# Expert stage of a two-block transformer kernel: TensorE in program order, its parts reordered, output product in quarters, token low parts on POOL

## The chip, the cores and the metric

The kernel runs on one core of one Trainium2 chip. The metric is the time of one execution on the device in microseconds (us), from the first to the last instruction and what lies around it. Its engines work side by side: TensorE (PE) does matrix products and transposes, VectorE (DVE) and ScalarE (ACT) work element by element, GpSimd (POOL) does a few elementwise operations and issues small loads, SyncE (SP) issues the loads of the weights.

## The reference

256 tokens of width 1024 go through two blocks of two layers each. A layer of the first block is: a scale and a shift made from a condition vector (adaLN), a mixer of attention, retention and mLSTM, an output product, a layer norm, and a mixture of 16 experts of which each token takes two; then a second layer norm. A layer of the second block is another mixer and a dense feed-forward part, and at its end a gated product of the layer's own input `p` (`ple`). The change lies in the first block:

```python
mod = (c_act @ w_ada[l] + b_ada[l])[:, None, :]
sh_m, sc_m, g_m, sh_f, sc_f, g_f = jnp.split(mod, 6, axis=-1)
...
x = layer_norm(DEEPNORM_ALPHA * x + (1.0 + g_m) * mix, ln_mix_g[l], ln_mix_b[l])
h = x * (1.0 + sc_f) + sh_f
...
hid = jax.nn.silu(jnp.einsum('td,edf->tef', h, w_gate)) * jnp.einsum('td,edf->tef', h, w_up)
hid = hid * gate[:, :, None].astype(hid.dtype)
return jnp.einsum('tef,efd->td', hid, w_down)
...
e = p[l] @ w_ple_up[l]
```

## The kernel before

Tokens lie in two halves `t` of 128, widths in two halves `c` of 512. Products that must be exact take a value as a high and a low part: `split` (L382) makes the high part on ACT and subtracts it from the value on DVE.

The class `Flow` (`te`) issues every matmul (L88) and transpose (L92). Pieces of work that may be mixed in are generators started with `te.start`; each `te.tick()` in a loop lets them run on as far as a planned time (the number that they yield) allows, and `te.settle` runs one to its end. A scheduler then orders each engine's instructions once more, by priorities, among those that are ready by its own estimate; on PE the order of the code is not binding. Buffers are handed out in the order of the code.

The weights come through `Stream`: SP loads them in a fixed order of use into a ring of ten buffers (`wf`) of 1 MB each; a buffer comes free when the code calls `free` or `free_raw` and PE has read it. A layer's experts take 48 such pieces.

A layer of the first block ends its mixer with `out_product` (L911), which sums four parts of the mixed values into two accumulators for each token half, and calls `done(t, c, ps)` for each finished quarter. `done` (L1131) makes the residual and the statistics, and behind the second quarter of a half the layer norm, and starts `moe_enter`: it transposes the normed tokens, multiplies them by the router, and keeps them as high and low parts (L1188 to L1192). Routing and ranking give each token its slot: an expert has 64 slots, two experts make a pair `q`, and a pair has 128 rows. A branch leaves for a slow way if a token has no slot.

Then the expert stage of `moe` follows. `gather(h)` brings the tokens into the slots (eight groups of four matmuls); `slots` transposes the slot matrix `P` to `PT`; `up(q)` multiplies the pair's rows by gate and up weights, 16 matmuls in which the pair's two experts alternate on two halves of 64 columns each; the result is gated to `hid` on ACT and DVE; `turn` transposes `hid` to `d`; `down(q)` is eight matmuls of the same alternating kind; `add(q)` brings the result, as high and low parts `yh` and `yl`, back to the tokens with eight matmuls. In before the loop runs up(q), down(q-1), turn, while add is a task that waits for 4.2 planned us and is then mixed in matmul by matmul. In layer 1 a further task, `ple_up(1)` (L1528), multiplies the loaded `p` by its weights; it belongs to the second block and stores its result by an SP DMA. `leave` ends the stage with the second layer norm.

Of the kernel before, what the change touches and what calls it, by code (L numbers as in the profile page):

```python
# [72 lines left out]
class Flow:  # L73
# [4 lines left out]
    def __init__(self, tc):  # L78
        self.tc, self.now, self.tasks, self.inside = tc, 0.0, [], False

# [3 lines left out]
    def matmul(self, out, lhsT, rhs, us=None, **k):  # L84
        if us is None:
            us = math.prod(rhs.shape[1:]) * (4 if rhs.dtype == F32 else 1) / 2400.0
        self.spend(max(us, 0.027))
        return self.tc.nc.tensor.matmul(out, lhsT, rhs, **k)  # L88

    def transpose(self, out, src, ident):  # L90
        self.spend(0.107)
        return self.tc.nc.tensor.transpose(out, src, ident)  # L92
# [113 lines left out]
class Build:  # L206
    def __init__(self, tc, A, out, es):
# [11 lines left out]
        self.NB4 = 13  # L219
        self.stream = Stream(self, 10, 4, 6)  # L220
# [301 lines left out]
    def ada(self, n):  # L522
# [3 lines left out]
        for _ in range(n):  # L526
# [18 lines left out]
            if k0 == 6:  # L545
                end = self.te.start(self.ada_end(l, r, row))
        return end
# [147 lines left out]
    def mix1(self, l, hs, done):  # L695
        nc = self.nc
        te, tick = self.te, self.tick
        with ExitStack() as es:
# [202 lines left out]
            return self.out_product(("out", l), mixh, mixl, (0, 1, 3, 2), lambda q: te.settle(need[q]), done)  # L901
# [9 lines left out]
    def out_product(self, key, mh, ml, order, need, done):  # L911
# [211 lines left out]
    def block1(self, l, hs):  # L1123
# [7 lines left out]
        def done(t, c, ps):  # L1131
# [3 lines left out]
            if t == 0 and c == 0:  # L1135
                e.gB = [self.bcast(self.gate[l][i]) for i in range(2)]
                self.router(l, e)
                e.lg = self.sc([128, 2, 16])
                e.xT = [None, None]
                e.xs, e.back = [], []  # L1140
# [10 lines left out]
        self.mix1(l, hs, done)  # L1151
# [13 lines left out]
    def moe_enter(self, l, e, t, xn):  # L1165

        nc, te = self.nc, self.te
        yield 4.6 if t == 0 else 0.5
# [20 lines left out]
        for c in range(2):  # L1189
            cs = slice(512 * c, 512 * c + 512)  # L1190
            self.split(h[:, cs], lw[:, cs], xn[:, cs])
        e.xs.append((h, lw))  # L1192

    def back(self, l, e, t):
# [8 lines left out]
        for k in range(8):  # L1203
            te.matmul(e.out[t][k // 4][:, spread(k % 4)], e.xT[t][:, k], self.identa,
                      start=k % 4 == 0, stop=False)
            if k == 3:
                yield 1.6

# [81 lines left out]
    def moe(self, l, e, xn):  # L1290
# [4 lines left out]
        with ExitStack() as es:  # L1295
# [37 lines left out]
            gather(0)  # L1333
            gt = self.gates(e)
            gsp = self.sc([128, 8, 2])
            for q in range(8):
                for t in range(2):
                    te.matmul(gsp[:, q], P[t].bitcast(F32)[:, q * 128:(q + 1) * 128], gt[:, t, 2 * q:2 * q + 2],
                              start=t == 0, stop=t == 1)
            gsl = S([128, 8], "m_gsl")  # L1340
            for a in range(2):
# [676 lines left out]
```

## Time and profile before

| | |
|---|---|
| time, median of 3 runs | 1476.96 us (1475.59 to 1484.74) |
| profiled execution, its own time | 1477.39 us |
| its span, first to last instruction | 1475.6 us |
| mean granted TensorE clock | 0.963 of full speed |
| PE busy | 1381.2 us, 94% |
| DVE busy | 879.1 us, 60% |
| ACT busy | 657.7 us, 45% |
| POOL busy | 83.2 us, 6% |
| DMA, mean over the span | 216 GB/s |

The first block fills the span to about 790 us, its two expert stages lie at 254 to 406 and at 618 to 778. The second block takes the rest. How it is read: the page gives the busy share of each engine; the timeline lists instructions in order with the idle time ahead of each and the engine that ended it; a table of stretches gives busy time, granted clock and DMA rate between two times. On PE consecutive rows overlap a little, since the matmuls are pipelined, and each matmul of full-precision inputs of `up` and `down` stands twice, once for each of its passes.

### The profile page before, as it was taken

Reading aid. Unit: us, or ns where it says so; the run is one execution under the profiler, and the core shown is the slowest. Engines: PE = TensorE matmul, PEld = TensorE weight load, DVE = VectorE, ACT = ScalarE, POOL = GpSimd, SP = SyncE. Lnnn points to the kernel's source line nnn. Section 1 sums busy time; section 2 is a strip of 40 time slices with the busy share of each in tenths; the row PEclk is TensorE's granted clock in tenths of the full one; section 3 lists DMA queues with packets and bytes.
Section 4 is the critical chain, followed back from the end, with each engine's and each line's share of the span. In section 5 each row is a group of like instructions: output and inputs, shape, how many; then the busy total and the mean of one; then the engine's idle time right before and its main releaser. Section 6 shows DMA issues by size and latency. Waiting matters only on the chain.

```text
span 1475.6 us, 18521 instructions
## 1 busy us (share of the span) xinstructions
PE 1381.2 (94%) x6642; PEld 972.5 (66%) x6642; DVE 879.1 (60%) x2094; ACT 657.7 (45%) x1317; POOL 83.2 (6%) x107
## 2 busy tenths in 40 slices
PE   4899997999979999799998998999999999999997
PEld 1667676633356767563336886888877887788885
DVE  1787567121288776412228787655569787665567
ACT  1536233111233542411116756555467866555554
POOL 3210001100001010000002000000001000000000
PEclk7899997999989999899999999999999999999999
DMA  9776597399746666539956533565655543556550
GB/s 334 250 270 217 211 327 286 127 411 412 253 171 235 228 220 243 200 118 410 411 222 225 177 95 128 167 191 184 193 176 166 176 119 114 171 172 193 188 204 28
DMA packets 129887, 318.12 MB, mean 216 GB/s; under 512 B 10199, under 2 KB 67711, under 8 KB 119546
## 3 DMA queue, kind: packets, MB, share of 16 engines
q1 hardware_dynamic: 125546, 304.96, 58.5%
q0 software_dynamic: 4240, 11.88, 2.7%
q8 instruction: 56, 0.92, 0.3%
q14 instruction: 45, 0.37, 0.1%
HBM read 313.64 MB, written 3.17 MB: 215 GB/s over the span
## 4 chain that ended last, share of the span: by engine, by line
PE 47%; DVE 6%; ACT 3%; issue 1%; DVEq 0%; ACTq 0%
PE sc L88 22%; PE mm L88 17%; PE tp L88 6%; PE tp L92 3%; DVE w L368 3%; ACT w L367 1%; DVE b L1603 0%; ACT junk L1599 0%; DVE b L1611 0%; ACT qz L693 0%; DVE b L384 0%; DVE rs_t L403 0%; DVE y L1401 0%; ACT b L383 0%; DVE b L1511 0%
## 5 line engine op out<-in xcount | busy, mean ns | idle before, releaser
L88 PE MATMUL mm<-w,b 128*128 128x512 f32 (+3 forms) x1920 | 454.6, 384 | 7.1 <-DVE b L601 4.1
L88 PEld LDWEIGHTS mm<-w,b 128*128 128x128 f32 x1920 | 342.7, 192 | 72.7 <-issue 8.1
L88 PE MATMUL sc<-w,b 128*128 128x512 f32 x1056 | 251.8, 394 | 3.7 <-DVE b L384 3.2
L368 DVE SCALAR_TENSOR_TENSOR w<-wf,vt,w 128x512 fp32r<-128x512 f32 (+2 forms) x304 | 199.3, 705 | 48.7 <-ACT w L367 48.5
L88 PEld LDWEIGHTS sc<-w,b 128*128 128x128 f32 x1056 | 197.1, 189 | 45.3 <-DVE b L384 4.1
L367 ACT ACTIVATE w<-wf,vt 128x512 fp32r<-128x512 f32 (+2 forms) x304 | 188.9, 681 | 46.8 <-PE sc L88 18.3
L362 DVE TENSOR_TENSOR w<-wf,w 128x1024 fp32r<-128x1024 f32 (+1 forms) x140 | 168.7, 1224 | 42.0 <-ACT w L361 41.5
L361 ACT CAST w<-wf 128x1024 fp32r<-128x1024 f32 (+1 forms) x140 | 140.7, 1033 | 71.4 <-PE mm L88 36.6
L88 PE MATMUL tp<-wf,X 128*64 128x512 f32 x512 | 132.9, 616 | 0.0
L88 PE MATMUL mm<-w,fh 128*128 128x512 f32 x352 | 110.5, 395 | 0.0
L88 PEld LDWEIGHTS tp<-wf,X 128*64 128x64 f32 x512 | 37.2, 140 | 70.3 <-issue 67.7
L88 PE MATMUL sc<-wf,d 128*64 128x512 f32 x256 | 79.2, 599 | 0.0
L1370 DVE SCALAR_TENSOR_TENSOR hid<-hid,m_gsl,tp 128x256 f32<-128x256 f32 x16 | 7.7, 481 | 119.7 <-ACT hid L1369 119.7
L88 PEld LDWEIGHTS mm<-w,fh 128*128 128x128 f32 x352 | 64.6, 188 | 12.5
L88 PE MATMUL mm<-w,fl 128*128 128x512 f32 x176 | 68.7, 390 | 0.0
L92 PE MATMUL tp<-identr,b 128*128 128x128 f32 (+3 forms) x236 | 40.3, 307 | 29.9 <-DVE b L1515 13.7
L1369 ACT ACTIVATE hid<-tp 128x256 f32<-128x256 f32 x16 | 6.1, 384 | 138.1 <-PE tp L88 138.1
L88 PE MATMUL sc<-wf,cact 128*32 128x512 f32 x384 | 53.0, 653 | 13.0 <-DMA wf<-in_w_ada_dram 9.1
L1895 DVE SCALAR_TENSOR_TENSOR f<-sc,en_r,sl 128x256 f32<-128x256 f32 x44 | 21.2, 481 | 68.4 <-ACT sl L1893 68.4
L92 PEld LDWEIGHTS tp<-identr,b 128*128 128x128 f32 (+3 forms) x236 | 31.1, 167 | 45.1 <-DVE b L1515 15.4
L1893 ACT ACTIVATE sl<-sc,en_r 128x256 f32<-128x256 f32 x44 | 20.5, 465 | 80.5 <-PE sc L88 80.5
L88 PE MATMUL sc<-b,b 128*128 128x512 f32 x128 | 41.4, 466 | 11.9 <-DVE m_gsum L1279 4.7
(402 smaller groups left out, 1649.9 us busy)
## 6 DMA issues: line engine op xcount, KB each, us to landing
wf<-in_w_ada_dram SPq DMA_DIRECT2D x48, 1024.0 KB, 6.9
wf<-in_w_ffn_in_dram SPq DMA_DIRECT2D x88, 512.0 KB, 4.8
wf<-in_w_in_dram SPq DMA_DIRECT2D x32, 1024.0 KB, 6.1
wf<-in_w_gate_dram SPq DMA_DIRECT2D x64, 512.0 KB, 7.6
wf<-in_w_up_dram SPq DMA_DIRECT2D x64, 512.0 KB, 8.8
wf<-in_w_down_dram SPq DMA_DIRECT2D x32, 1024.0 KB, 9.5
wf<-in_w_ffn_out_dram SPq DMA_DIRECT2D x22, 1024.0 KB, 4.9
wf<-in_w_out_dram SPq DMA_DIRECT2D x12, 1024.0 KB, 7.1
```

Of the source, the lines that this page charges most:

```text
L88: return self.tc.nc.tensor.matmul(out, lhsT, rhs, **k)
L92: return self.tc.nc.tensor.transpose(out, src, ident)
L361: nc.scalar.copy(wh, w)
L362: nc.vector.tensor_tensor(wl, w, wh, OP.subtract)
L367: nc.scalar.activation(wh[:, k], w[:, k], AF.Copy, scale=g)
L368: nc.vector.scalar_tensor_tensor(wl[:, k], w[:, k], g, wh[:, k], op0=OP.mult, op1=OP.subtract)
L1369: nc.scalar.activation(hid, gu[:, 0], AF.Silu)
L1370: nc.vector.scalar_tensor_tensor(hid, hid, gsl[:, q:q + 1], gu[:, 1], op0=OP.mult, op1=OP.mult)
L1893: nc.scalar.activation(sl, gu[:, :256], AF.Silu, scale=r)
L1895: nc.vector.scalar_tensor_tensor(f, gu[:, 256:], r, sl, op0=OP.mult, op1=OP.mult)
```

## The change

Five things are done, all in the first block.

- `Flow` has a switch `strict`. While it is on, `behind` makes each PE instruction depend on the one issued before it, so the scheduler keeps the order of the code on PE. It is on from the first gather to the last add of each expert stage.
- The code of the stage is reordered. The slot gates come behind up(0) instead of behind gather(0). For each q the order is up(q), down(q-1), add(q-2), turn; for q = 1 slots take the place of the add. add is no task any more: its eight matmuls stand together, by token halves, and the elementwise part that makes `yh` and `yl` stands in down. At the end come down(7), add(6), add(7), and in layer 1 ple_up(1) is started only then.
- `out_product` finishes its last two parts quarter by quarter for both token halves (before: one half at once, then two quarters), and frees the last weights later.
- A hook `before` runs ahead of these quarters: it settles the adaLN tasks that are still open, and makes the broadcasts and the router's operands, which `done` made in its first call.
- `moe_enter` makes the low parts of the tokens by a POOL subtract instead of DVE's, and yields 2.4 planned us instead of 4.6. `warm` is added and not called.

```diff
+    def behind(self, made):
+
+        if self.strict and self.last:
+            self.tc.add_manual_dep(made.ins, self.last, mybir.DependencyInfo(
+                mybir.DependencyClass.NoSync, mybir.DependencyReason.DATA))
+        self.last = made.ins.name
+        return made
...
-        part(2, 0)
-        part(3, 0)
-        done(0, 0, ps[0])
-        done(0, 1, ps[0])
-        for c in range(2):
-            part(2, 1, (c,), c == 1)
-            part(3, 1, (c,), c == 1)
-            done(1, c, ps[1])
+        if before:
+            before()
+        for t in range(2):
+            for c in range(2):
+                part(2, t, (c,), t == 1 and c == 1)
+                part(3, t, (c,), t == 1 and c == 1)
+                done(t, c, ps[t])
...
+        def before():
+            te.settle(*self.ada_ends)
+            e.gB = [self.bcast(self.gate[l][i]) for i in range(2)]
+            self.router(l, e)
...
-        yield 4.6 if t == 0 else 0.5
+        yield 2.4 if t == 0 else 0.5
...
-            self.split(h[:, cs], lw[:, cs], xn[:, cs])
+            nc.scalar.copy(h[:, cs], xn[:, cs])
+            nc.gpsimd.tensor_tensor(lw[:, cs], xn[:, cs], h[:, cs], OP.subtract)
...
-                return te.start(add(q))
-
-            def add(q):
-
                 yh, yl = self.b4([128, D], F32R), self.b4([128, D], F32R)
...
-                yield 4.2
+                ys[q] = yh, yl
+
+            def add(q):
+
                 for t in range(2):
                     for c in range(2):
                         cs = slice(512 * c, 512 * c + 512)
-                        for y in (yh, yl):
+                        for i, y in enumerate(ys[q]):
                             te.matmul(out[t][c], PT[:, q, t * 128:(t + 1) * 128], y[:, cs], start=False,
...
+            te.strict = True
+            gather(0)
             for q in range(8):
-                hid = up(q)
+                gu = up(q)
                 if q == 0:
+                    slot_gates()
+                    hid = gated(q, gu)
                     slots((0, 2))
                     gather(1)
-                elif q == 1:
-                    slots((4, 6))
-                    self.rows(l, x)
-                if q:
-                    end = down(q - 1, d)
+                else:
+                    hid = gated(q, gu)
+                    down(q - 1, d)
+                    if q == 1:
+                        slots((4, 6))
+                        self.rows(l, x)
+                    else:
+                        add(q - 2)
                 d = turn(hid)
...
-            end = down(7, d)
+            down(7, d)
+            add(6)
+            add(7)
+            te.strict = False
             fill = te.start(self.ple_up(1), 1) if l else None
-            te.settle(end)
```

Three places show how instructions stand in a row. The first is PE in layer 0's expert stage, one of the later pairs. `tp<-wf,X` are matmuls of an up, `sc<-wf,d` of a down, `tp<-identr,hid` the two transposes of a turn, `mm<-b,PT` the adds into four accumulators. Before:

```order
L88 MATMUL tp<-wf,X 64x512 x15
L88 MATMUL sc<-wf,d 64x512 x2
L92 MATMUL tp<-identr,hid 128x128 x2
L88 MATMUL sc<-wf,d 64x512 x6
L88 MATMUL mm_2070<-b_3754,PT 128x512
L88 MATMUL mm_2072<-b_3754,PT 128x512
L88 MATMUL mm_2070<-b_3755,PT 128x512
L88 MATMUL tp<-wf,X 64x512
L88 MATMUL mm_2072<-b_3755,PT 128x512
L88 MATMUL mm_2071<-b_3754,PT 128x512
L88 MATMUL mm_2073<-b_3754,PT 128x512
L88 MATMUL mm_2071<-b_3755,PT 128x512
```

After:

```order
L93 MATMUL tp<-identr,hid 128x128 x2
L89 MATMUL tp<-wf,X 64x512 x16
L89 MATMUL sc<-wf,d 64x512 x8
L89 MATMUL mm_1991<-b_3610,PT 128x512
L89 MATMUL mm_1991<-b_3611,PT 128x512
L89 MATMUL mm_1992<-b_3610,PT 128x512
L89 MATMUL mm_1992<-b_3611,PT 128x512
L89 MATMUL mm_1993<-b_3610,PT 128x512
L89 MATMUL mm_1993<-b_3611,PT 128x512
L89 MATMUL mm_1994<-b_3610,PT 128x512
L89 MATMUL mm_1994<-b_3611,PT 128x512
L93 MATMUL tp<-identr,hid 128x128 x2
```

Before, the add's matmuls stand in the middle of an up (one ahead, 15 behind), and the turn in the middle of a down, after two of its eight. After, each part stands whole.

The second place is PE at the end of layer 1's expert stage. `sc<-wf,b` are ple_up's matmuls and the transposes of `b_7440` (before) and `b_7508` (after) turn its tokens; `b_7471` (before), `b_7457` and `b_7487` (after) are the normed tokens that the second block's first projection, `mm<-w,b 128x384`, takes. Before:

```order
L88 MATMUL mm_5622<-b_7430,PT 128x512
L92 MATMUL tp<-identr,b_7440 128x128 x2
L88 MATMUL mm_5620<-b_7431,PT 128x512
L92 MATMUL tp<-identr,b_7440 128x128 x2
L88 MATMUL sc<-wf,b_7440 128x512 x2
L88 MATMUL mm_5622<-b_7431,PT 128x512
L88 MATMUL sc<-wf,b_7440 128x512 x6
L92 MATMUL tp<-identr,b_7471 128x128 x8
L88 MATMUL mm_7644<-w_7336,b_7490 128x384 x2
```

After:

```order
L89 MATMUL mm_5572<-b_7431,PT 128x512
L93 MATMUL tp<-identr,b_7508 128x128 x2
L93 MATMUL tp<-identr,b_7457 128x128 x4
L93 MATMUL tp<-identr,b_7508 128x128 x2
L89 MATMUL sc<-wf,b_7508 128x512
L93 MATMUL tp<-identr,b_7457 128x128 x4
L89 MATMUL sc<-wf,b_7508 128x512
L93 MATMUL tp<-identr,b_7487 128x128 x4
L89 MATMUL sc<-wf,b_7508 128x512
L93 MATMUL tp<-identr,b_7487 128x128 x4
L89 MATMUL sc<-wf,b_7508 128x512 x5
L89 MATMUL mm_7644<-w_7336,b_7476 128x384 x2
```

Before, ple_up's work stands between the last adds and ahead of all transposes of the normed tokens. After, it begins behind the last add, its first transposes are ahead of the normed tokens' and its matmuls between and behind those, ahead of the projection.

The third place is POOL's queue from layer 1's branch on, up to the second block's small loads; `in_p_dram` is ple_up's load, and the instruction on qs waits for the last add in both kernels. Before:

```order
L418 DMA b_6951<-in_ln_ffn_g_dram 128x1024
L418 DMA b_6953<-in_ln_ffn_b_dram 128x1024
L1532 DMA b_7440<-in_p_dram 128x2x256
L1562 DMA qs<-in_k_qs_dram 128x768
L1628 MEMSET qz 128x3072
L1630 MEMSET qc 128x1536
L1642 DMA lb<-in_gmlp_ln_g_dram 128x256
L1643 DMA lb<-in_gmlp_ln_b_dram 128x256
L1645 DMA P<-in_w_spatial_dram 128x4x128
L1647 DMA bs<-in_b_spatial_dram 4x128
L1558 DMA b_7610<-in_k_dist_dram 128x1024
L418 DMA b_7618<-in_g_post_mix_dram 128x1024
```

After:

```order
L428 DMA b_6977<-in_ln_ffn_g_dram 128x1024
L428 DMA b_6979<-in_ln_ffn_b_dram 128x1024
L1593 DMA qs<-in_k_qs_dram 128x768
L1659 MEMSET qz 128x3072
L1661 MEMSET qc 128x1536
L1673 DMA lb<-in_gmlp_ln_g_dram 128x256
L1674 DMA lb<-in_gmlp_ln_b_dram 128x256
L1676 DMA P<-in_w_spatial_dram 128x4x128
L1678 DMA bs<-in_b_spatial_dram 4x128
L1563 DMA b_7508<-in_p_dram 128x2x256
L1589 DMA b_7610<-in_k_dist_dram 128x1024
```

The load of `p` stood ahead of qs and the two memsets, and stands now behind them and behind four small loads. Further ahead on POOL, before the branch of each layer, the four subtracts of the token low parts are new. On SP, six weight pieces of the second block's projection stand ahead of the first store of ple_up's result, where two stood.

## Rows read from the trace of the kernel before

**Rows 1.** The page, busy time of each engine, share of the span, instructions.
```profile
PE 1381.2 (94%) x6642; PEld 972.5 (66%) x6642; DVE 879.1 (60%) x2094; ACT 657.7 (45%) x1317; POOL 83.2 (6%) x107
```

**Rows 2.** Timeline of PE, layer 0's expert stage: start, us, engine, line, operation, count [idle before].
```profile
302.81 4.51 PE L88 MATMUL tp<-wf,X 128*64 128x512 f32 x20
...
312.27 3.60 PE L88 MATMUL sc<-wf,d 128*64 128x512 f32 x16
...
316.24 4.51 PE L88 MATMUL tp<-wf,X 128*64 128x512 f32 x20
...
334.11 2.11 PE L88 MATMUL mm<-b,PT 128*128 128x512 f32 x8
...
357.08 0.51 PE L92 MATMUL tp<-identr,hid 128*128 128x128 f32 x2
357.52 3.65 PE L88 MATMUL sc<-wf,d 128*64 128x512 f32 x12
361.74 1.23 PE L88 MATMUL mm<-b,PT 128*128 128x512 f32 x3 [0.57 <-ACT b L383]
...
373.37 0.50 PE L92 MATMUL tp<-identr,hid 128*128 128x128 f32 x2
```

**Rows 3.** Timeline of PE, start and end of the same stage.
```profile
259.09 1.07 PE L88 MATMUL tp<-wf,X 128*64 128x512 f32 x2
...
381.59 6.65 PE L88 MATMUL tp<-wf,X 128*64 128x512 f32 x29
...
395.48 1.93 PE L88 MATMUL sc<-wf,d 128*64 128x512 f32 x4
...
404.24 1.46 PE L88 MATMUL mm<-b,PT 128*128 128x512 f32 x4 [0.72 <-ACT b L383]
...
415.99 1.97 PE L92 MATMUL tp<-identr,b 128*128 128x128 f32 x8 [8.43 <-DVE b L1515]
```

**Rows 4.** Timeline of PE, end of layer 1's expert stage and what follows.
```profile
751.47 6.65 PE L88 MATMUL tp<-wf,X 128*64 128x512 f32 x29
...
777.77 5.31 PE L88 MATMUL sc<-wf,b 128*128 128x512 f32 x12
788.30 1.97 PE L92 MATMUL tp<-identr,b 128*128 128x128 f32 x8 [5.22 <-DVE b L1515]
790.09 5.02 PE L88 MATMUL mm<-w,b 128*128 128x384 f32 x15
```

**Rows 5.** Stretch of 40 us by engine, clock, DMA; DMA rates 300 to 400, 40 slices.
```profile
320.00:360.00 40.00, 39.17 (x156) 14.19 (x153) 6.97 (x11) 4.73 (x10) 0.00 (x0) 1.00 1.02 414
...
GB/s 419 403 385 416 421 410 392 411 419 426 423 405 405 410 405 411 426 415 405 411 410 413 428 416 406 408 403 413 421 423 419 417 328 42 210 101 328 95 305 72
```

**Rows 6.** Timeline of PE, layer 0 between the output product and the routing.
```profile
225.60 2.77 PE L88 MATMUL sc<-wf,cact 128*32 128x512 f32 x22
230.80 1.82 PE L92 MATMUL tp<-identr,b 128*128 128x128 f32 x8 [2.42 <-DVE b L1121]
```

**Rows 7.** Two stretches: us, busy time by engine, PEclk (granted clock), DMA share, GB/s.
```profile
231.15:241.39 10.24, 10.24 (x50) 10.00 (x48) 7.75 (x20) 6.30 (x13) 1.05 (x2) 0.50 1.02 411
787.52:794.35 6.83, 6.04 (x20) 5.30 (x21) 6.83 (x20) 4.86 (x12) 0.00 (x0) 0.50 1.03 377
```

**Rows 8.** POOL: its largest group by form (mean ns), and two timeline rows.
```profile
L677 POOL TENSOR_TENSOR ro<-ra,rb 128x512 f32<-128x512 f32 x12 | 16.9, 1411 | 113.3 <-DVE rb L676 94.8 <-PE sc L92 17.0 <-DVE rs_z L393 1.5
...
430.65 1.93 POOL L677 TENSOR_TENSOR ro<-ra,rb 128x320 f32<-128x320 f32 x1 [31.10 <-DVE rb L676]
...
434.99 0.87 POOL L677 TENSOR_TENSOR ro<-ra,rb 128x320 f32<-128x320 f32 x1 [2.11 <-DVE rb L676]
```

**Rows 9.** Timeline of POOL behind layer 1's stage; landing time of the p loads (L1532).
```profile
778.49 0.57 POOL L1562 DMA_DIRECT2D qs<-in_k_qs_dram  x1 [59.02 <-DVE w L368]
...
784.77 0.53 POOL L1647 DMA_DIRECT2D bs<-in_b_spatial_dram  x1
...
DMA to landing us min/median/max: 4.8/5.9/6.9
```

More of the change, by code (lines that the diff above doesn't have):

```diff
@@ L79, in __init__ @@
         self.tc, self.now, self.tasks, self.inside = tc, 0.0, [], False
+        self.strict, self.last = False, None
     def spend(self, us):
@@ L546, in ada @@
                 end = self.te.start(self.ada_end(l, r, row))
+                self.ada_ends.append(end)
         return end
@@ L693, in transp_z, with mix1 @@
             self.nc.scalar.copy(dst[r * w:(r + 1) * w, r::parts], t[r * w:(r + 1) * w, :n])
-    def mix1(self, l, hs, done):
+    def mix1(self, l, hs, done, before):
         nc = self.nc
@@ L900, in mix1 @@
             need = {0: at, 1: at, 3: ml, 2: rt}
-            return self.out_product(("out", l), mixh, mixl, (0, 1, 3, 2), lambda q: te.settle(need[q]), done)
+            return self.out_product(("out", l), mixh, mixl, (0, 1, 3, 2), lambda q: te.settle(need[q]), done, before)
     def to_mix(self, y, dh, dl, n):
@@ L909, in to_mix, with out_product @@
         self.split(dh, dl, tps.rearrange("p n t c -> p n (t c)"))
-    def out_product(self, key, mh, ml, order, need, done):
+    def out_product(self, key, mh, ml, order, need, done, before=None):
         ps = [[self.mm(i=t) for _ in range(2)] for t in range(2)]
@@ L1134, in done @@
                 r[t] = self.b1.tile([128, D], F32, name="r", bufs=1)
[L1135 to L1140, printed above, removed]
             s = slice(512 * c, 512 * c + 512)
@@ L1149, in done @@
                 e.task = te.start(self.moe_enter(l, e, t, xn[t]))
-        self.mix1(l, hs, done)
+        def before():
+            te.settle(*self.ada_ends)
+            e.gB = [self.bcast(self.gate[l][i]) for i in range(2)]
+            self.router(l, e)
+            e.lg = self.sc([128, 2, 16])
+            e.xT = [None, None]
+            e.xs, e.back = [], []
+        self.mix1(l, hs, done, before)
         return self.moe(l, e, xn)
@@ L1207, in back, with warm @@
                 yield 1.6
+    def warm(self, n):
+        ps = self.tp([128, 512])
+        for i in range(n):
+            self.te.matmul(ps[:, :128], self.onesb, self.onesb, us=0.056)
     def first(self, v, m, n, name):
@@ L1331, in gather, with slot_gates @@
                         nc.scalar.activation(X[:, k, hs], ps, AF.Identity, bias=e.B[:, k:k + 1], scale=e.G[:, k:k + 1])
[L1333 to L1339, printed above, removed]
-            gsl = S([128, 8], "m_gsl")
-            for a in range(2):
-                nc.vector.tensor_copy(gsl[64 * a:64 * a + 64], gsp[64 * a:64 * a + 64, :, a])
+            gsl = S([128, 8], "m_gsl")
+            def slot_gates():
+                gt = self.gates(e)
+                gsp = self.sc([128, 8, 2])
+                for q in range(8):
+                    for t in range(2):
+                        te.matmul(gsp[:, q], P[t].bitcast(F32)[:, q * 128:(q + 1) * 128], gt[:, t, 2 * q:2 * q + 2],
+                                  start=t == 0, stop=t == 1)
+                for a in range(2):
+                    nc.vector.tensor_copy(gsl[64 * a:64 * a + 64], gsp[64 * a:64 * a + 64, :, a])
             PT = T([128, 8, 256], "PT", F32R)
```

10 lines of the change are left out of this document (6 added, 4 removed).

## The prediction

> **What bounds the kernel now.** I began with the busy shares of the page: TensorE (PE) is busy 94% of the span, POOL 6% [rows 1]. So time goes only where PE waits, or where its own work gets shorter. The change touches the first block alone, above all its two expert stages, so I read the timeline of PE there next.
>
> Inside a stage PE hardly waits, but it is not equally fast. One pair of experts is up(q), down(q-1), an add and a turn. An early pair goes from 302.81 to 316.24, which is 13.43 us; a late one, from turn to turn, from 357.08 to 373.37, which is 16.29 us, though it holds the same instructions [rows 2]. They differ in how the runs of 64-column matmuls (`tp<-wf,X` of up, `sc<-wf,d` of down) are cut. The trace lists two passes for each matmul, so an up has 32 rows and a down 16. A whole down and its turn take 3.97 us (312.27 to 316.24), the turn about 0.45 of it: 0.22 for a row. In the late pairs the turn falls after four rows of the down and the add in the middle of an up, and the 12 rows left of the down take 3.65, 0.30 each [rows 2]; two rows by themselves take 1.07 [rows 3]. My reading: the two column halves run side by side while instructions alternate, and an odd cut leaves one half running alone. The late add also starts after 0.57 us of waiting for ACT.
>
> The last add of layer 0 ends at 404.24+1.46 = 405.70, and PE's next work on the path comes at 415.99, after 8.43 us of waiting for a layer norm [rows 3]. In layer 1 the add ends at about 777.8, as the rest of ple_up's matmuls starts, and the second block's first projection matmul stands at 790.09 [rows 4].
>
> The third view was the weights. While PE runs the late pairs the DMA share is 1.02 at 414 GB/s [rows 5]; 1 MB (1.0486 million bytes) takes 2.53 us at that rate and a pair's six pieces 15.2 us. That is less than 16.29 but more than 13.43: the stream holds PE back as soon as PE is faster and the ring of ten buffers has run empty.
>
> **The change, part by part.**
>
> *Program order in the stage.* Removed are the cuts. A pair then holds 32 rows of up at 0.22 (7.04), 16 of down (3.52), an add of eight (2.11) and the turn (0.45) [rows 2]: 13.1 us. The five pairs from up(2) to up(7) take 381.59-302.81 = 78.8 now [rows 2, 3] and would take 65.5.
>
> Is the weight stream fast enough? In before it runs full until about 382 (the rates by slices of 2.5 us fall at the 33rd) [rows 5], while the last down starts at 395.48 [rows 3]: 13 us of lead. The pairs take 13.3 of it and the start of the stage 2.5 (below). The first refill comes some 4 us earlier, by my estimate, since up(0) is no longer stretched by gathers. That leaves about 2 us of waiting, near up(7). I count 65.5+2 = 67.5, so **-11.3 in each layer**; bounds 0 and 4 us of waiting.
>
> From up(7) to the end: 7.04+3.52+2.11+0.45+3.52+2.11+2.11 = 20.9, against 405.70-381.59 = 24.1 in layer 0 [rows 3] and 777.8-751.47 = 26.3 in layer 1, where ple_up's matmuls lie between the adds [rows 4]: **-3.2 and -5.4**. The elementwise chain of the last y hides behind add(6).
>
> The start of the stage has the same odd cuts: two rows take 1.07 (259.09) [rows 3] where 0.44 would do. I count about seven that cost 0.4 to 0.6 us: **-3.5** in each layer. Against it, slots and turn of the second expert now stand right behind work that they wait for: **+1**, an estimate of two waits like the 0.57 in [rows 2].
>
> *Output product by quarters and the settled tasks.* The quarters stood nearly so on PE before. The adaLN matmuls of layer 0 (2.77 us the largest lot, at 225.60) [rows 6] and their two DVE adds leave the place ahead of token half 0 and come between the halves. What half 0 gains, half 1 pays back on a PE that is busy 10.24 of 10.24 us there, at half clock [rows 7].
>
> *Low parts of the tokens on POOL.* DVE is relieved of four subtracts a layer. POOL does 128x512 with two inputs in 1.41 us on average, and gather(0) reads these results. Both may slow each other down: POOL's 128x320 addition took 1.93 us while DVE subtracted, and 0.87 a little later [rows 8]. So each of the four may hold a two-input DVE instruction for about 1 us, in the norm and routing chain that PE waits for. Both edits of the front together: **+2 in layer 0** (bounds -2 and +6, the second being about four times 1.41), **+1.5 in layer 1**, which has no adaLN part (-1 and +4).
>
> The Trainium skill, "SBUF — State Buffer", section "SBUF: two separate sides", has this as a rule: the port pair that DVE and GpSimd share is an exclusive lock, so a DVE operation with two SBUF inputs and a GpSimd operation that reads SBUF block each other for a whole instruction. The stretched row agrees with it; taken to the letter it gives the upper bounds just named, and 1456+4+2.5 = 1462.5 in all.
>
> *The tail of layer 1.* In before ple_up's matmuls run between the adds and in the norm's gap, which ends at 788.30 [rows 4]; they cost next to nothing. After, ple_up starts behind the last add. On POOL its load now stands behind qs, which waits for the last add, and behind two memsets and four small loads, which in before run from 778.49 to 784.77+0.53 = 785.30; from issue to landing such a load takes 4.8 to 6.9 us [rows 9]. It arrives 12.3 to 14.4 us behind the last add, where the norm is ready for its first transposes after 788.30-777.8 = 10.5. The p transposes stand ahead of those on PE, and ple_up's 16 passes, 7.1 us at the 5.31 for 12 [rows 4], stand ahead of the first projection matmul. DVE has no room either: it is busy 6.83 of 6.83 us there [rows 7]. 7.1, about 3 of waiting and 1 for the copies between is **+11**; bounds +3 (most of ple_up fits into the wait) and +16 (its 5 us more if PE does it at half clock). SP gains a little: six weight pieces instead of two stand ahead of the store that waits for ple_up.
>
> Sum: layer 0, 2-3.5+1-11.3-3.2 = -15.0; layer 1, 1.5-3.5+1-11.3-5.4+11 = -6.7. That is -21.7 against the profiled execution's 1477.39, so 1455.7, rounded **1456**; the median of the three runs, 1476.96, is 0.4 lower, which changes nothing.
>
> **Rivals.**
>
> *Better: tail and front cost next to nothing.* Tail +3 instead of +11, both fronts 0: -8-3.5, so 1445. For it: POOL's small loads may be issued faster than their spans say. Against: PE has little other waiting behind 790 in which ple_up could hide.
>
> *The weights bind.* If the lead is gone by up(2), a pair is 15.2 us, five are 76, and each layer saves 2.8 instead of 11.3: 1456+17 = 1473. For it: the DMA share is 1.02 already [rows 5]. Against: ten pieces lie ready at the start, and 13 us of lead remain in before.
>
> *Both ends at their upper bounds.* Tail +16, fronts +6 and +4: 1456+5+4+2.5 = 1467.5. For it speaks the stretched POOL row [rows 8].
>
> *Slower: the clock falls in the stage.* PE waits for weights in each pair, and the granted clock drops to half, 1.2 GHz. Idles of 0.57 us leave it at 1.00 [rows 2, 5], while a stretch of 10.24 us at 0.50 follows a wait of 2.42 [rows 6, 7]. If the level stood at half for half of the work from up(2) on, the 65.5+20.9 = 86.4 us would take 86.4/0.75 = 115.2; that is +28.8, less the 2 of waiting, 26.8 per layer: 1510. It decides once a wait of over 2 us stands ahead of each up from the third on. Against: at half clock PE is slower than the stream, and the waits vanish.
>
> **How the numbers follow.** Forecast 0.62; better 0.12; weights bind 0.13; ends at the upper bounds 0.06; clock 0.07. About 1% (1462 to 1492) is what a measurement of this kernel can tell from no change. Faster by more: forecast and better, 0.74. Within: weights and ends, 0.19. Slower: 0.07. The forecast's own range, with the bounds of tail, fronts and waiting not all at one end, is 1447 to 1464; with better and the ends it is **1441 to 1469** and holds 0.80.
>
> **What would show it.** Steps right: turns 13 us apart from up(2) to up(7), no two-pass row that lasts 1 us; full DMA rate until shortly before the last down; waits for weights of some 2 us, near the end only; in layer 1 the p load issued about 7 us behind the last add, and the first projection matmul some 23 us behind it (12.3 now); POOL subtracts of 1.4 us or more with stretched DVE rows beside them. Wrong: turns 15.2 apart with PE waiting for `wf` (weights bind), a granted clock of 0.50 inside the stage (slower case), or a projection that starts within 16 us of the last add (better).

## The result and the profile after

The changed kernel takes 1458.55 us (median of 4 runs, 1453.35 to 1459.71), the kernel before, timed beside it, 1477.24 (1475.59 to 1484.74). The ratio is 0.9857, interval [0.9822, 0.9892]: about 1.4% faster, 2.6 us above the forecast of 1456.0 and inside its range. The profiled execution took 1459.71 us; its span is 1457.9, 17.7 less than the 1475.6 of before.

The page's busy times, as in [rows 1]:

```profile
PE 1352.6 (93%) x6642; PEld 977.2 (67%) x6642; DVE 872.4 (60%) x2086; ACT 655.9 (45%) x1317; POOL 93.4 (6%) x115
```

PE has the same 6642 instructions and is busy 28.6 us less (1381.2 before). The span shrank by 17.7, so PE waits some 11 us more than it did. The timeline of PE shows where, cut at landmarks that both kernels have: the mixer's last four transposes (`tp<-identr,y`, so the output product lies behind them), the first gather (`sc<-b,b`, 32 rows), the start of up(2) and of up(7), the end of the last add, and the first matmul of the second block's projection.

| piece, us | before | after | difference | forecast |
|---|---|---|---|---|
| layer 0: mixer's last transposes to first gather (front) | 39.5 | 44.5 | +5.0 | +2 |
| first gather to up(2) | 48.6 | 46.2 | -2.4 | -2.5 |
| up(2) to up(7) | 78.8 | 67.1 | -11.7 | -11.3 |
| up(7) to end of last add | 24.1 | 23.7 | -0.4 | -3.2 |
| layer 1: front | 36.3 | 39.0 | +2.7 | +1.5 |
| first gather to up(2) | 54.9 | 50.2 | -4.6 | -2.5 |
| up(2) to up(7) | 78.8 | 66.9 | -11.9 | -11.3 |
| up(7) to end of last add | 26.4 | 23.7 | -2.7 | -5.4 |
| last add to first projection matmul (tail) | 12.2 | 25.0 | +12.8 | +11 |

These make -13.2. The rest of the -17.7 lies outside them: 1.0 ahead of the first front, 0.7 in the gap behind layer 0, 2.4 in the second block's projection, which starts 12.8 later behind the last add and ends 10.4 later, and 0.4 in small amounts.

The stage of layer 0, as in [rows 2, 3], in the timeline of PE (start, us, engine, line, operation, out<-in, count, [idle before <-releaser]):

```profile
304.29 7.16 PE L89 MATMUL tp<-wf,X 128*64 128x512 f32 x32
311.21 3.67 PE L89 MATMUL sc<-wf,d 128*64 128x512 f32 x16
314.81 2.11 PE L89 MATMUL mm<-b,PT 128*128 128x512 f32 x8
316.76 0.39 PE L93 MATMUL tp<-identr,hid 128*128 128x128 f32 x2
...
329.49 0.39 PE L93 MATMUL tp<-identr,hid 128*128 128x128 f32 x2
...
365.46 3.65 PE L89 MATMUL sc<-wf,d 128*64 128x512 f32 x14 [1.23 <-DMA wf<-in_w_down_dram]
...
371.02 0.39 PE L93 MATMUL tp<-identr,hid 128*128 128x128 f32 x2
...
386.19 0.39 PE L93 MATMUL tp<-identr,hid 128*128 128x128 f32 x2
387.32 3.65 PE L89 MATMUL sc<-wf,d 128*64 128x512 f32 x16 [0.74 <-ACT d L1402]
```

Every part stands whole: 32, 16, 8 and 2 rows. From turn to turn a pair with its weights there is 12.73 us (316.76 to 329.49). Then the weights are late: a down waits 1.23 us for its piece, and the last pair takes 15.17 (371.02 to 386.19), the rate of six pieces in 15.2. The turn before the last down is followed by 0.74 us of waiting for ACT.

The front of layer 0, against [rows 6]: the timelines of PE, DVE and POOL.

```profile
225.63 1.28 PE L93 MATMUL tp<-identr,b 128*128 128x128 f32 x8 [3.42 <-DVE b L1131]
...
228.87 3.62 PE L89 MATMUL sc<-wf,cact 128*32 128x512 f32 x10
...
234.67 1.93 PE L89 MATMUL sc<-wf,cact 128*32 128x512 f32 x6
...
240.24 1.94 PE L89 MATMUL sc<-wf,cact 128*32 128x512 f32 x16
242.12 1.23 PE L93 MATMUL tp<-identr,b 128*128 128x128 f32 x8
...
258.09 11.25 PE L89 MATMUL sc<-b,b 128*128 128x512 f32 x32 [6.55 <-PEq L1323]
```

```profile
227.80 2.21 DVE L1147 SCALAR_TENSOR_TENSOR r<-b,r 128x512 f32<-128x512 f32 x2
...
236.66 0.69 DVE L554 TENSOR_TENSOR adarow<-sc,adarow 128x512 f32<-128x512 f32 x1 [5.45 <-PE sc L89]
...
249.44 1.10 DVE L1236 TENSOR_TENSOR f2e<-f2e,f2r 128x32 f32<-128x32 f32 x1
```

```profile
227.61 1.26 POOL L1204 TENSOR_TENSOR b<-b,b 128x512 fp32r<-128x512 f32 x1 [36.85 <-ACT b L1203]
...
249.23 1.26 POOL L1204 TENSOR_TENSOR b<-b,b 128x512 fp32r<-128x512 f32 x1 [3.69 <-ACT b L1203]
```

Three things are to be seen. The adaLN matmuls (`sc<-wf,cact`, 7.5 us in three lots) stand between the transposes of half 0 (225.63) and those of half 1 (242.12), where the granted clock is 0.57 on average (228.90 to 242.10). DVE's add on them (L554) stands ahead of half 1's norm with 5.45 us of waiting. And beside POOL's subtracts two DVE rows are stretched: L1147 takes 2.21 for two (1.28 before), a 128x32 operation 1.10. In the timeline of DVE before that one is

```profile
248.28 0.19 DVE L1217 TENSOR_TENSOR f2e<-f2e,f2r 128x32 f32<-128x32 f32 x1
```

The tail of layer 1, against [rows 4, 9], in the chain of waits (start, us, what):

```profile
746.02 4.08 PE mm L89 x16
...
750.38 0.54 POOL qs L1593
750.92 2.67 POOL qz L1659
753.59 1.31 POOL qc L1661
...
757.16 6.29 DMA b<-in_p_dram
...
763.49 1.97 PE tp L93 x8
```

It is the path that the forecast wrote down: last add, qs, two memsets, four small loads, then the p load, which lands 6.29 us later, and only then PE. The first projection matmul comes at 775.09, 25.0 behind the last add.

### The profile page after: what moved, and what is told of

It reads as the page before. It is cut to its first block, busy times and chain, and to the rows that moved or that the text cites. A ratio compares the mean times of both kernels' runs of the same rounds, so it can differ in the third digit from the quotient of the medians.

```text
span 1457.9 us, 18528 instructions
## 1 busy us (share of the span) xinstructions
PE 1352.6 (93%) x6642; PEld 977.2 (67%) x6642; DVE 872.4 (60%) x2086; ACT 655.9 (45%) x1317; POOL 93.4 (6%) x115
## 4 chain that ended last, share of the span: by engine, by line
PE 47%; DVE 5%; ACT 3%; DMA 2%; issue 1%; POOL 0%; DVEq 0%; ACTq 0%
PE sc L89 22%; PE mm L89 17%; PE tp L89 4%; PE tp L93 3%; DVE w L378 2%; DMA wf<-in_w_down_dram 2%; ACT w L377 1%; DVE b L1634 0%; DMA b<-in_p_dram 0%; DVE b L1642 0%; ACT qz L704 0%; ACT junk L1630 0%; DVE b L394 0%; DVE rs_t L413 0%; POOL qz L1659 0%
## 5 line engine op out<-in xcount | busy, mean ns | idle before, releaser
L372 DVE TENSOR_TENSOR w<-wf,w 128x1024 fp32r<-128x1024 f32 (+1 forms) x140 | 168.6, 1223 | 42.0 <-ACT w L371 40.2
L89 PE MATMUL tp<-wf,X 128*64 128x512 f32 x512 | 117.4, 596 | 0.0
L89 PEld LDWEIGHTS tp<-wf,X 128*64 128x64 f32 x512 | 38.7, 137 | 65.8 <-issue 63.9
L93 PE MATMUL tp<-identr,b 128*128 128x128 f32 (+3 forms) x236 | 39.9, 307 | 41.7 <-DMA b<-in_p_dram 13.4
L89 PE MATMUL sc<-wf,d 128*64 128x512 f32 x256 | 63.7, 595 | 6.5 <-DMA wf<-in_w_down_dram 5.0
L89 PE MATMUL sc<-wf,cact 128*32 128x512 f32 x384 | 56.4, 682 | 11.2 <-DMA wf<-in_w_ada_dram 7.3
```

The source lines that it names most:

```text
L89: return self.behind(self.tc.nc.tensor.matmul(out, lhsT, rhs, **k))
L93: return self.behind(self.tc.nc.tensor.transpose(out, src, ident))
L372: nc.vector.tensor_tensor(wl, w, wh, OP.subtract)
```

## The experiments

All but the last are edits of the changed kernel. Differences of a piece are read in the profiled execution between the landmarks of the table. "Ratio" is that to the kernel before, timed in the same session.

### Does the order of the parts alone bring the gain?

The chain of orders is never switched on; all else of the change stays.

```
-            te.strict = True
+            te.strict = False
```

> The changed kernel without the dependency chain (strict never on): the code of the stage is written in the new order, the scheduler may move PE's instructions. Theory (the chain brings the gain, not the order of the code): the scheduler puts the turn into the down and the add into the up again, late pairs take 16.0 to 16.5 us as before and nothing waits for weights: 15 to 20 us of the gain are gone, 1472 to 1480 us. Rival (the code's order carries most of it): pairs of 14 us or less, 1462 us or less.

Measured: 1488.42 us (1478.97 to 1495.14, 10 runs), ratio 1.0046 [1.0016, 1.0077]. PE's timeline in layer 0, one pair:

```profile
361.57 0.51 PE L93 MATMUL tp<-identr,hid 128*128 128x128 f32 x2
362.01 3.65 PE L89 MATMUL sc<-wf,d 128*64 128x512 f32 x12
366.23 1.22 PE L89 MATMUL mm<-b,PT 128*128 128x512 f32 x3 [0.57 <-ACT b L393]
367.38 1.07 PE L89 MATMUL tp<-wf,X 128*64 128x512 f32 x2
...
377.86 0.50 PE L93 MATMUL tp<-identr,hid 128*128 128x128 f32 x2
```

The pair takes 16.29 again, with every pattern of [rows 2]: 12 rows of a down behind the turn, the wait for ACT, two rows that take 1.07. Without the chain the rewritten code is cut as before, and all the rest of the change costs about 10 us, which is more than the expectation had.

### What does one cut cost?

The chain stays; add(q-2) is put inside the up, behind the 11th of its 16 matmuls (an odd cut, as shown) or, in the second kernel, behind the 12th (`a == 1`).

```
+                        if mid is not None and k == 5 and a == 0:
+                            add(mid)
...
-                    else:
-                        add(q - 2)
```

> The changed kernel with add(q-2) moved into up(q), behind the 11th of its 16 matmuls, so between the two column halves of one step (an odd cut); program order stays. Theory (the halves run side by side while they alternate, an odd cut leaves one half alone): the first three pairs of the steady stretch, 12.73 us apart now, take 13.1 to 13.4. The pairs that go at the rate of the weights stay near 15.2. Rival (only the number of changes between kinds of matmul costs): this kernel and the one with the even cut take the same.

> As the kernel with the odd cut, but the add stands behind the 12th matmul of up, so behind a whole step of both halves (an even cut). Theory: the first three pairs take 12.7 to 12.9, within 0.2 us of the changed kernel. Rival (any cut costs): as much as with the odd cut, 13.1 or more.

One timing each: 1469.1 and 1459.01 us. PE's timeline in layer 0, the odd cut:

```profile
321.07 0.51 PE L93 MATMUL tp<-identr,hid 128*128 128x128 f32 x2
321.51 5.36 PE L89 MATMUL tp<-wf,X 128*64 128x512 f32 x22
...
335.00 0.51 PE L93 MATMUL tp<-identr,hid 128*128 128x128 f32 x2
```

and the even one:

```profile
316.87 0.50 PE L93 MATMUL tp<-identr,hid 128*128 128x128 f32 x2
317.30 5.37 PE L89 MATMUL tp<-wf,X 128*64 128x512 f32 x24
...
329.94 0.50 PE L93 MATMUL tp<-identr,hid 128*128 128x128 f32 x2
```

A pair takes 13.93 with an odd cut and 13.07 with an even one, against 12.73 with none: 1.2 and 0.33 us. So cuts cost time, and odd ones 0.86 more, as the reading of one half running alone wants: ahead of the odd cut 22 rows of the up take 5.36 us, as long as the 24 ahead of the even one (5.37). Both cost more than was expected. The 3.56 us that a late pair of before lost (16.29 to 12.73) are then 1.2 for the odd cut, 0.57 for ACT, and 1.8 that is left for the turn inside a down. This last part was not measured by itself; the 12 rows behind such a turn take as long as the 16 of a whole down (3.65 and 3.60, [rows 2]), so some of them ran alone too, although the turn stands behind an even number of matmuls.

The price of a pair is not that of the stage. From the first gather to the last add the even cut takes 134.9 and 139.4 us, less than the change with its 137.0 and 140.9: it has one pair at the rate of the weights (15.20 in layer 0) where the change has two. The odd cut takes 137.8 and 142.2, and no pair of its steady stretch is slower than 13.97.

### How much do the weights hold back?

From the fourth pair on, half of each gate and up piece is loaded and used twice. This kernel leaves out half of those weights and so computes something else; it only prices the waits.

```
+                    m = 512 if q >= 3 else 1024
...
+                h = 2 if q >= 3 else 4
```

> The changed kernel, but from the fourth pair on only half of each gate and up weight piece is loaded and the matmuls read that half twice; the same instructions on PE, a third less to load for these pairs (so the experts' result is another). Theory (the last pairs go at the rate of the weights: turns 12.73, 12.75, 13.56, 15.22, 15.17 us apart, waits of 1.25 for down weights): all pairs take 12.7 to 12.8, the end of the stage has no wait for weights, 5 to 6 us less in each layer, 1447 to 1449 us. Rival (the longer pairs come from PE's own order or from ACT): pairs stay at 15, within 2 us of 1458.

Measured: 1440.74 us (1435.13 to 1445.14), ratio 0.9752 [0.9714, 0.979]. PE's timeline, layer 0, the last two turns of pairs and the last down:

```profile
366.73 0.39 PE L93 MATMUL tp<-identr,hid 128*128 128x128 f32 x2
...
379.46 0.39 PE L93 MATMUL tp<-identr,hid 128*128 128x128 f32 x2
380.60 3.65 PE L89 MATMUL sc<-wf,d 128*64 128x512 f32 x16 [0.75 <-ACT d L1404]
```

The late pairs take 12.73 to 12.75, no row of the stage waits for DMA, and from the start of up(2) to the last turn layer 0 is 5.7 us shorter, layer 1 5.6. So the weights cost 5.7 a layer where 2 was forecast; the 0.75 for ACT stays. The total fell by 18, more than twice 5.7; 5 of it are the tail, which with fewer loads was 20.0 instead of 25.0. This kernel therefore prices the waits by its stage and not by its total.

### Can the stream start earlier?

While PE gathers, the ring is full and nothing is loaded: SP's queue waits there up to 19.0 us at a time for the ups of PE, which free the buffers. This is the page's row of rates over 256 to 400 us of the changed kernel, 3.6 us a slice:

```profile
GB/s 15 306 121 0 7 330 389 412 32 0 0 225 415 415 409 415 426 402 412 419 413 405 410 409 427 408 409 411 424 416 397 409 422 420 423 365 343 403 341 380
```

From the 13th slice on it is full to the end; ahead of it lie two holes, at the first gather and at gather(1). The edit moves gather(1) behind the add of the fourth pair, so that the first ups come earlier.

```
-                    gather(1)
...
+                    if q == 3:
+                        gather(1)
```

> The changed kernel with gather(1), whose columns only up(4) to up(7) read, moved from the first pair to behind the add of the fourth. PE does the same work. Theory (the last pairs wait because the weight stream stood still while PE gathered with the ring full): the loads run on, all pairs but the one with the gather take 12.7 to 12.8, no wait for down weights; from the first gather to the last add 5 to 6 us less in each layer, 1446 to 1450 us. Rival (the stream is short in total, wherever its pauses lie): waits for weights come elsewhere in the stage, 1455 us or more.

Measured: 1455.29 us (1451.13 to 1462.35), ratio 0.9845 [0.9812, 0.9879]. No weight wait is left, and the four pairs behind the moved gather take 12.73 to 12.75. But from the first gather to the last add the gain is 3.0 in layer 0 and 6.0 in layer 1: in layer 0 up(1) now runs partly at half clock (9.29 us instead of 7.09; the granted clock is 0.50 from 282.61 to 287). The total cannot be told from that of the change; in the profiled execution 4 us of the gain went into a stretch at half clock in the mixer of layer 1 (last section).

### The tail

ple_up is started ahead of the last two adds again.

```
             down(7, d)
+            fill = te.start(self.ple_up(1), 1) if l else None
             add(6)
...
-            fill = te.start(self.ple_up(1), 1) if l else None
```

> The changed kernel with one edit: ple_up(1) is started ahead of add(6) instead of behind add(7), so that its load of p stands ahead of qs on POOL again. Theory (the tail costs 12.8 us because PE waits 13.40 us for p and then does ple_up on the path): the load lands before the stage ends, the wait ahead of PE's next transposes falls to the norm's own 5 to 6 us, ple_up's 7 us lie in that gap, and the first projection matmul stands 13 to 15 us behind the last add instead of 25.0: 10 to 12 us less, some 1447 us. Rival (the projection waits for its weights and their scaling on ACT and DVE anyway): it starts at most 3 us earlier, 1455 us or more.

Measured: 1445.06 us (1441.13 to 1455.59), ratio 0.9775 [0.974, 0.981], 13.5 less than the change. PE's timeline behind the last add:

```profile
752.97 4.12 PE L89 MATMUL mm<-b,PT 128*128 128x512 f32 x16
...
758.04 6.17 PE L89 MATMUL sc<-wf,b 128*128 128x512 f32 x14
...
768.39 1.65 PE L89 MATMUL mm<-w,b 128*128 128x384 f32 x4
```

The p load is issued ahead of qs again, ple_up's matmuls fill the time in which the norm is made, and the tail is 11.3 us. The chain does not matter here: with the chain off and ple_up late (the first experiment) the tail was 24.2.

### The front: three edits apart

Low parts made by DVE's split as before; the output product and the hook as before (the code of the old lines is put back); the planned time in `moe_enter` as before.

```
-            nc.scalar.copy(h[:, cs], xn[:, cs])
-            nc.gpsimd.tensor_tensor(lw[:, cs], xn[:, cs], h[:, cs], OP.subtract)
+            self.split(h[:, cs], lw[:, cs], xn[:, cs])
```

> The changed kernel with the low parts of the tokens made by DVE again, as before. Theory (POOL's subtracts hold DVE's two-input instructions): the two residual additions of half 1 take 1.28 us instead of 2.21, the routing's 128x32 operation 0.19 instead of 1.10; against that DVE gets its 0.69 us subtracts back, one of them inside the routing chain. Sum per layer between -1.5 and +0.5, so 1456 to 1459 us. Rival (taking work from DVE is worth it): the first gather starts 1.5 us or more later in each layer, 1461 us or more.

```
-        if before:
-            before()
-        for t in range(2):
-            for c in range(2):
+        part(2, 0)
+        part(3, 0)
+        done(0, 0, ps[0])
```

> The changed kernel with the output product and the hook as before: half 0 whole, no settling of the adaLN tasks ahead of it. Theory (in layer 0 DVE stands 5.45 us at the adaLN addition, which is ahead of half 1's norm in its queue and waits for PE): that wait goes, half 0 starts some 5 us later, half 1's norm 2 to 4 us earlier; the first gather of layer 0 starts 2 to 6 us earlier (258.09 now), layer 1's within 1 us of now: 1453 to 1457 us. Rival (quarters and the early half 0 carry the front): the first gather of layer 0 starts at the same time or later, 1459 us or more.

```
-        yield 2.4 if t == 0 else 0.5
+        yield 4.6 if t == 0 else 0.5
```

> The changed kernel with the planned wait of moe_enter at 4.6 again instead of 2.4. Theory (this number, not the settling, put the adaLN matmuls behind half 0's transposes, and POOL's subtracts ahead of half 1's residual): adaLN stands ahead of half 0's transposes again, DVE's wait of 5.45 us ahead of half 1's norm falls under 1.5, and from the mixer's last transposes (tp of y) to the first gather it is 39 to 42 us in layer 0 (44.46 now) and 36 to 38 in layer 1 (39.05 now): 4 to 7 us less, 1452 to 1455. Rival (POOL alone makes the front longer): 43 us or more in layer 0, 1457 or more.

| kernel | us (range) | ratio | front, layer 0 | front, layer 1 |
|---|---|---|---|---|
| before | 1477.24 | 1 | 39.5 | 36.3 |
| changed | 1458.55 (1453.35 to 1459.71) | 0.9857 [0.9822, 0.9892] | 44.5 | 39.0 |
| low parts on DVE | 1457.56 (1451.26 to 1463.4) | 0.9882 [0.9842, 0.9922] | 40.2 | 38.7 |
| output product as before | 1459.2 (1451.2 to 1462.76) | 0.9862 [0.9825, 0.9899] | 44.4 | 40.7 |
| planned 4.6 us again | 1453.46 (1452.88 to 1456.82) | 0.9832 [0.9791, 0.9873] | 41.9 | 36.3 |

Single executions differ by themselves: in the changed kernel and the six kernels of this document that leave its front as it is, the front takes 42.8 to 44.8 us in layer 0 and 39.0 to 40.7 in layer 1.

My theory of the output product fell: with its old order the adaLN matmuls still stand behind half 0 and DVE's add still waits 5.44 us, and both fronts are as long as those. It is the number in `moe_enter` that moves them. With 4.6 they are done ahead of half 0, as in [rows 6]; PE's timeline of that kernel:

```profile
225.43 2.77 PE L89 MATMUL sc<-wf,cact 128*32 128x512 f32 x22
230.17 1.29 PE L93 MATMUL tp<-identr,b 128*128 128x128 f32 x8 [1.97 <-DVE b L1131]
```

Both fronts are 2.5 to 2.7 shorter. But the place of the adaLN matmuls is not the whole reason. Layer 1, which has none there, gains as much. And where DVE makes the low parts they stand behind half 0 just as well, with a front of 40.2; the first kernel of the next part, which has 4.6 as well, comes to 39.3, only 0.9 less. What the number changes in layer 1 stands in PE's timeline, at the transposes of half 1, with 2.4 and with 4.6:

```profile
588.36 1.95 PE L93 MATMUL tp<-identr,b 128*128 128x128 f32 x8 [2.95 <-DVE b L1131]
...
584.89 1.20 PE L93 MATMUL tp<-identr,b 128*128 128x128 f32 x8 [1.27 <-DVE b L1131]
```

With 2.4 PE waits 2.95 us there, and from 588.36 to 594.00 the granted clock is 0.51: the 16 router rows that follow take 3.60 us. With 4.6 the wait is 1.27, the granted clock from 584 to 590 is 0.97, and they take 1.96. Of the 2.7 us 1.3 lie ahead of these transposes and 1.6 between them and the ranking's first matmul.

With the low parts on DVE the front of layer 0 is 4.2 shorter, of layer 1 0.3. About 1.8 of the 4.2 are the two stretched rows, and 1.85 lie ahead of the first gather, in PE's timeline of that kernel:

```profile
250.70 10.20 PE L89 MATMUL sc<-b,b 128*128 128x512 f32 x32 [4.70 <-DVE m_gsum L1297]
```

With POOL's subtracts this wait was 6.3 to 6.8 in each of the nine kernels that have them, and put down to PE's own branch; with DVE's it was 4.7 to 5.1. Why the place of the subtracts moves it is open. The totals of these three kernels don't separate them from the change; the pieces do.

### All repairs together, and the chain alone

Two kernels join ple_up early, low parts on DVE and 4.6 us; the second also has gather(1) late.

> The changed kernel without what cost time at its ends: ple_up(1) started ahead of add(6), low parts on DVE, planned wait 4.6; the stage in program order and the output product in quarters stay, gather(1) where the change has it. Theory (the stage alone is worth 28 to 30 us against the kernel before, and the other parts took 17 of it back): 1438 to 1444 us; from the mixer's last transposes to the first gather 39 to 40.5 us in layer 0 and 36 to 37 in layer 1. Rival (the front's and the tail's losses come from the shorter stage itself): 1448 us or more.

> The changed kernel with four edits together: ple_up(1) started ahead of add(6), low parts of the tokens on DVE, planned wait 4.6, gather(1) late. Theory (four separate losses that add up): 10 us of the tail, 5 of the front in layer 0 and 2.7 in layer 1, 11 in the two stages: 1428 to 1436 us, faster than the changed kernel by some 26. Rival (the gains overlap, since the tail's wait shrinks by itself when the weights are earlier): 1437 to 1445 us.

Measured: 1442.11 us (1435.59 to 1452.03), ratio 0.9771 [0.9736, 0.9807], and 1438.94 us (1435.33 to 1445.55), 0.9731 [0.9704, 0.9758]. In the first, both fronts are those of before (39.3 and 36.0) and the tail is 11.3. The second has the lowest median of all; the two intervals overlap, so what gather(1) brings on top is not shown by the totals. It also fell short of what was hoped and landed in the range of the rival. Its front of layer 1 is 42.3, but this is the landmark: the 7.28 us of waiting ahead of its first gather stand in the other kernels in two parts, the second behind the gather's first rows (2.67 and 3.79 in the change). From the mixer's last transposes to up(0) it takes 52.7 us, the first kernel 50.9 and the change 54.3. In the profiled execution the mixer of layer 1, from the last add of layer 0 to those transposes, is 4.3 us longer than in the first (179.1 and 174.8).

The last kernel is the one before, with nothing but the chain, from the first gather to the last down. ple_up, the front and the order in which the parts are written stay as they were.

```
+            te.strict = True
             gather(0)
...
             end = down(7, d)
+            te.strict = False
```

> The kernel before with nothing but the dependency chain of PE in the expert stage (strict on from the first gather to the last down); the code keeps its old order, in which the add's eight matmuls stand in two lots of four in the middle of the next up, each behind a whole step of both halves, and the turn behind the down. Theory (the chain alone brings most of the gain, since it keeps the cuts even; an even cut costs 0.33 us): pairs of 13.3 to 13.6 us, front and tail as before, 20 to 25 us less than before in all: 1453 to 1458 us, the same as the whole change. Rival (the new order of the code is needed, PE would stand in order behind adds that wait for ACT): pairs of 14.5 us or more, 1463 us or more.

Measured: 1449.19 us (1448.77 to 1450.18), ratio 0.9801 [0.976, 0.9842]: its four executions (1448.77 to 1450.18) all lie below those of the whole change, though the two intervals of the ratio overlap a little, and it brings more than was expected of it. PE's timeline, layer 0, one pair:

```profile
312.31 0.51 PE L93 MATMUL tp<-identr,hid 128*128 128x128 f32 x2
312.74 4.51 PE L89 MATMUL tp<-wf,X 128*64 128x512 f32 x20
317.18 1.20 PE L89 MATMUL mm<-b,PT 128*128 128x512 f32 x4
...
325.76 0.51 PE L93 MATMUL tp<-identr,hid 128*128 128x128 f32 x2
```

Its add cuts the up twice, behind the 10th and the 12th matmul, both even, and a pair takes 13.45. But the change's 12.73 cannot be kept up, since the weights come at 15.2 a pair: from the first gather to the last add this kernel takes 138.0 and 143.9 us, the change 137.0 and 140.9. Writing the parts in another order is worth some 4 us in both layers together; the chain is worth 28 by itself, and all the rest of the change, this order included, takes 10 back.

## Why the prediction was right, point by point

- **Program order in the stage.** Right: the gain is there and comes from the cuts (first two experiments). -11.3 a layer was forecast from up(2) to up(7), and -11.7 and -11.9 came. Two errors cancelled in it. The pair of 13.1 was too long, since the rows of [rows 2] that it was added up from still held the ends of their runs: 12.73 each, 1.9 less for five. And the waiting, taken as 2, is 3.3 in this stretch (two pairs are 0.83 and 2.49 above 12.73).
- **From up(7) to the end.** This is the term that was mis-sized: -3.2 and -5.4 forecast, -0.4 and -2.7 measured. The 20.9 us had no wait in them. The last pair still goes at the weights' rate, 2.44 above 12.73, and the last down waits 0.74 for ACT; less 0.37 for the shorter pair this makes 23.7, which is what came. The working counted the lead up to up(7) and let the stream be on time from there on. In all the weights cost 5.7 us a layer; the 13 us of lead were there, but the holes at the two gathers are not filled, as the ring is full by then.
- **Start of the stage.** -2.5 forecast, -2.4 in layer 0. Of the -4.6 in layer 1, 0.8 is PE's issue gap in the first gather, 4.56 before and 3.79 after.
- **The front.** Right in sign, too small: +5.0 and +2.7 instead of +2 and +1.5, inside the bounds. The step on POOL was right in kind, as the stretched rows show: about 0.9 us lost in each of two places. The Trainium skill, "SBUF — State Buffer", section "SBUF: two separate sides", calls the shared port an exclusive lock for a whole instruction; the 1.10 beside a POOL subtract of 1.26 agrees with it. The step "what half 0 gains, half 1 pays back" held to 0.7 us where DVE makes the low parts (40.2 against 39.5 before, with the adaLN matmuls behind half 0); beside POOL's subtracts 4.6 brought 2.5 in layer 0, and how much of that is the place of the adaLN matmuls is open. The prediction named the wrong edit for their place. The change of 4.6 to 2.4 stood in the diff and was given no price; in layer 1 it cost 2.7 by a wait and by the half clock behind it.
- **The tail.** Right in path and size: +12.8 for +11. The forecast's 3 us of waiting were more, since PE's first work behind the last add comes only with the p load, 13.4 us later, and the matmuls ran between the transposes in short lots. The upper bound of +16 counted 5 us more for ple_up at half clock, where doubling its 7.1 adds 7.1; the measured +12.8 lies below either.
- **The rivals.** "The weights bind" is true for the last two pairs of each layer, and so for one of the five it named. "The clock falls in the stage" did not happen: over 342.20 to 395.00, where PE waits 1.23 and 1.25 us for weights, the granted clock is 1.00. Tail and front were not cheap ("better"), and not at their upper bounds.

Sum by sum: layer 0 came to -9.5 where -15.0 was forecast, layer 1 to -3.7 where -6.7 was; 4.5 us of small gains outside, which the forecast did not have, left the profiled execution 4.0 above the sum. So it is in part luck that the total came within 2.6 us: the pieces alone were 8.5 short.

## What to carry to other kernels

When matmuls use half the array's columns and alternate halves, keep their runs whole in the order in which they are issued, and cut them, if at all, behind a full pair; then ask which stream becomes the bound, since beyond its rate a better order brings little. Take a change apart by its parts even where it wins: here the chain brought 28 us and the rest together gave 10 back, and a filler task that starts a few instructions too late, behind a queue that waits for the end of the stage, cost as much as five uncut pairs gain. A planner's number in a diff is an edit like any other, and has to be priced by what it moves.

## What the runs showed of the hardware

Cutting a run of 64-column matmuls that alternate cost 0.33 us a pair behind an even number of them (13.07 against 12.73) and 1.2 behind an odd one (13.93). I had expected next to nothing for the first.

Waits of 1.23 and 1.25 us in the stage and of 1.27 in layer 1's front (the kernel with 4.6) left the granted clock at 1.00 and 0.97; behind waits of 2.95 in that front and of 2.42 in layer 0 before [rows 6, 7] it was 0.51 and 0.50.

The granted clock can also fall while PE is busy all the time. In one execution of the kernel with late gathers, the table of stretches in the mixer of layer 1 (us, busy time of PE, PEld, DVE, ACT, POOL, granted clock, DMA share, GB/s):

```profile
520.00:522.00 2.00, 2.00 (x15) 1.67 (x14) 0.56 (x1) 1.60 (x3) 0.00 (x0) 1.00 0.80 328
522.00:524.00 2.00, 2.00 (x8) 1.29 (x7) 1.23 (x1) 0.78 (x3) 0.00 (x0) 0.65 0.00 0
524.00:526.00 2.00, 2.00 (x10) 2.00 (x9) 0.56 (x1) 0.02 (x1) 0.00 (x0) 0.50 0.00 0
```

PE is busy 2.00 of 2.00 us in each, with no wait ahead of the drop. The changed kernel keeps 1.00 over the same work:

```profile
512.63:536.63 24.00, 24.00 (x144) 16.32 (x144) 14.65 (x29) 8.00 (x17) 1.28 (x1) 1.00 0.52 179
```

In the first of the two the way from the transposes behind layer 0's stage to those at the front of layer 1 is 169.5 us, in the second 165.5. Single executions of one of the changed kernels lie some 4 to 16 us apart, and this is part of it, since some of the other profiled executions have 168 to 169 there as well. The clock of whole executions points the same way: with ple_up early the two of 1441 us had a mean granted clock of 0.973 and 0.974, the one of 1455.59 had 0.961. What brings the clock down in the mixer is open.
